# Order of the early gate operands and the first gate sums on VectorE

## The chip, the cores and the metric

The kernel runs on one core of a Trainium2 chip. The metric is the device time of one execution in microseconds, as the median over timed runs; the profile is of one further execution.

## The reference

Two layers of an encoder over 1024 tokens of 1024 features, in float32. Each layer is a token mixer (layer 0: multi-head latent attention, layer 1: differential attention), its output projection, and a SwiGLU part, both with a scaled residual and a layer normalisation:

```python
h = _layernorm(ALPHA * h + mix, ln_mix_g[i], ln_mix_b[i])
h = _layernorm(ALPHA * h + _swiglu(h, ffn_w_gu[i], ffn_w_down[i]), ln_ffn_g[i], ln_ffn_b[i])

def _swiglu(x, w_gu, w_down):
    gate, up = jnp.split(x @ w_gu, 2, axis=-1)
    return (jax.nn.silu(gate) * up) @ w_down
```

The hidden width D_FF is 2816, that is 22 blocks of 128.

## The kernel before

Engines: TensorE (PE in the profile) does the matmuls, VectorE (DVE), ScalarE (ACT) and GpSimd (POOL) the elementwise work, and the sync queue (SP) issues most transfers. Each engine, and the sync queue, takes its instructions in one fixed order. That order is not the order of the text: a planner replays the program against its own model of the durations and puts each instruction at the place where that model has it ready, with priorities (`tc.high_priority`) that lift some. The function `behind(i, j)` adds a constraint for the planner: instruction i comes after j on their engine; it adds no semaphore.

**Operands.** A float32 operand of a matmul is split into a high part (a cast on ScalarE, L503) and a low part (the rest, L504, on VectorE or GpSimd); a product is three matmuls per slice of 128 rows: high by high, high by low, low by high. `op_unit` (L508 on) makes such a pair; pairs turn over six buffers of the pool wp (tags wh and wl, three each), so the cast of a pair waits until TensorE has used up an older one.

**Output projection and normalisation.** The token blocks of 128 are taken in the order 6, 7, 4, 5, 2, 3, 0, 1 (`LAST_ORDER`); in layer 0 by `out_proj`, in layer 1 by the class `OutProj` (`rest`). For each block, `layer_norm` (from L163) makes two means (L166, L167), the squares on ScalarE (L170), the centring on VectorE (L176), the variance (L178), a power on GpSimd (L180), and the scaled and shifted output on VectorE (L183), which the sync queue stores (L184). In layer 1 y and z are one tile, so L176 overwrites what the squares read; in layer 0 they are two.

**Transposed sums.** `raw_x` (L463 on) transposes a finished block on TensorE into two PSUM banks (xTp). For the blocks 0 to 3 it then forms the sums of a Strassen-like scheme: L482 (b12), a copy of the second bank on ScalarE (L483, b22), L484 (b11), L485 and L486 (b21). L482 and L484 read the first bank, L483 and L485 the second. `raw_x` of a block is called after the `layer_norm` of the next; that of the last block, 1, is left over as `pending`, which `ffn` calls.

**Feed-forward part, gate stage.** `ffn` takes the 22 column blocks n of gate and up; with 7 products per block (numbered "1" to "7") in place of 8. Products 1 and 2 use the weights as they are; 3, 5, 6 and 7 use sums of weights. For the first six blocks (npre = 6), products 1 and 2 come early: `load_pre(n)` loads the two weights (tile gp, tag wr, two buffers) and makes the pairs op_gp, the low parts on GpSimd for n = 0 and 1 and on VectorE for n = 2 to 5; `gates(n)` runs the products of n and n+1 (PSUM tile ga, tag s, four banks, which `raw_x` uses too) in the order (n,1), (n+1,1), (n,2), (n+1,2), copies the first out (L608) and applies Silu to the second (L610), which frees the bank. The text goes: load_pre(0) to load_pre(3), gates(0), load(0), load(1) (tile gr, 1 MB each, L558), pending() with high priority, gates(2), the pairs of the transposed sums (t1, b22, t2, t3, t4), load_pre(4), load_pre(5), gates(4). `prepare(n, pr)` (L570 on) makes the operands of the other products from gr: for n = 0 and 1 the first gate sum a21 = a21 + a22 (L580), then a11 (L582), a12 (L584) and s3 (L588), each from the one before, and the pairs op_g. Their products go to the PSUM tiles gc and gb; L628 to L640 add them up.

Buffers that chain transfers to compute: the load of gp for n = 3 waits for the low parts of n = 1 on GpSimd, that for n = 4 for the low parts of n = 2, that for n = 5 for those of n = 3.

## Time and profile before

| | us |
|---|---|
| median of 3 runs | 2288.1 |
| lowest and highest | 2285.23, 2289.94 |
| the profiled execution | 2289.88 |
| its span, first to last instruction | 2288.1 |

Mean granted TensorE clock over the span: 0.997. TensorE is busy for 98% of the span, VectorE 68%, ScalarE 44%, GpSimd 38%.

In a row of a timeline stand the start, the duration, the engine, the line, the operation and its tiles, the number of instructions merged, and in brackets the idle time of the engine ahead of it with what ended that. In a row of the chain of waits stand start, duration, and what ran. In a row of windows stand the stretch, its length, the busy time (and instructions) of PE, PEld, DVE, ACT and POOL, then TensorE's clock, the DMA share and GB/s. Matmuls overlap in their pipeline: one lasts 0.39 us, and at full clock the next starts 0.23 us after it.

### The profile page before, as it was taken

How to read it: one execution, taken by the hardware profiler on the slowest of the kernel's cores; microseconds unless marked ns; L12 is line 12 of the kernel's file. 1: busy time of each engine (PE TensorE's matmuls, PEld its weight loads, DVE VectorE, ACT ScalarE, POOL GpSimd, SP SyncE). 2: the span in 40 equal slices, each digit the busy share in tenths (PEclk: the TensorE clock that was granted, in tenths of full speed). 3: DMA queues.
4: the chain of work that ended last, by engine and by line, in shares of the span. 5: the costliest groups of instructions: out<-in, count | busy, mean ns of one | idle time of the engine just before them, and what ended most of it. 6: DMA issues, size and time to landing. Idle time of an engine off the chain costs nothing.

```text
span 2288.1 us, 31118 instructions
## 1 busy us (share of the span) xinstructions
PE 2245.8 (98%) x11410; PEld 1913.3 (84%) x11410; DVE 1556.8 (68%) x2837; ACT 1015.4 (44%) x2097; POOL 864.0 (38%) x687
## 2 busy tenths in 40 slices
PE   8999999999999999999999999999999999999997
PEld 8999998878888887888889898988778888877886
DVE  5676665686666658677576666676776665668777
ACT  4455564342333324344465655564432333234353
POOL 2232341114444435555432423221024444436563
PEclk9999999999999999999999999999999999999998
DMA  5010125334444428444311212154254131338353
GB/s 201 14 35 31 41 72 198 140 132 151 151 152 179 151 103 331 184 179 149 106 45 31 70 28 66 33 200 155 92 175 143 69 138 69 138 115 317 132 205 119
DMA packets 105544, 288.28 MB, mean 126 GB/s; under 512 B 7968, under 2 KB 30112, under 8 KB 94896
## 3 DMA queue, kind: packets, MB, share of 16 engines
q1 hardware_dynamic: 100976, 275.87, 33.9%
q0 software_dynamic: 4416, 10.42, 1.6%
q8 instruction: 90, 1.47, 0.3%
q14 instruction: 62, 0.51, 0.1%
HBM read 205.00 MB, written 77.07 MB: 123 GB/s over the span
## 4 chain that ended last, share of the span: by engine, by line
PE 90%; DVE 4%; DMA 3%; issue 1%; ACT 1%; POOL 1%; SPq 0%; DVEq 0%; POOLq 0%; ACTq 0%
PE gb L549 14%; PE gc L549 10%; PE ga L549 10%; PE dw L818 7%; PE s_a L219 4%; PE zp_a L417 3%; PE dx L818 3%; PE s_b L219 3%; PE dv L818 3%; PE dy L818 3%; PE bp L145 3%; PE bp L143 3%; PE bp L144 3%; PE o_a L262 2%; PE o_b L262 2%; PE hq L1023 1%
## 5 line engine op out<-in xcount | busy, mean ns | idle before, releaser
L503 ACT CAST op_g<-gr 128x512 fp32r<-128x512 f32 x240 | 146.8, 621 | 370.1 <-PE gb L549 182.3
L504 POOL TENSOR_TENSOR op_g<-gr,op_g 128x512 fp32r<-128x512 f32 x104 | 146.6, 1415 | 247.9 <-ACT op_g L503 139.9
L504 DVE TENSOR_TENSOR op_h<-rh,op_h 128x512 fp32r<-128x512 f32 x154 | 162.5, 1083 | 63.7 <-ACT op_h L503 63.6
L549 PE MATMUL ga<-xh_m,op_g 128*128 128x512 f32 x512 | 168.2, 389 | 0.0
L503 ACT CAST op_h<-rh 128x512 fp32r<-128x512 f32 x154 | 92.9, 620 | 139.7 <-PE dx L818 38.0
L818 PE MATMUL dw<-op_w_t,op_h 128*128 128x512 f32 x660 | 151.3, 390 | 0.0
L818 PEld LDWEIGHTS dw<-op_w_t,op_h 128*128 128x128 f32 x660 | 123.5, 188 | 26.0 <-DVE op_h L504 0.4
L227 ACT ACTIVATE l_b<-l_b,mx_b 128x256 f32<-128x256 f32 (+7 forms) x128 | 99.4, 777 | 76.4 <-DVE mx_b L222 72.4
L818 PE MATMUL dx<-op_w_b,op_h 128*128 128x512 f32 x528 | 122.5, 391 | 7.4 <-ACT op_w_b L503 3.9
L1328 POOL TENSOR_SCALAR l_b<-l_b,rb,cst 128x128 f32<-128x128 f32 (+3 forms) x64 | 52.5, 820 | 204.4 <-DVE rb L1327 193.0
L504 POOL TENSOR_TENSOR op_w_t<-tt,op_w_t 128x512 fp32r<-128x512 f32 x66 | 98.7, 1499 | 80.7 <-ACT op_w_t L503 80.1
L818 PEld LDWEIGHTS dx<-op_w_b,op_h 128*128 128x128 f32 x528 | 98.5, 188 | 31.0 <-ACT op_w_b L503 4.7
L504 DVE TENSOR_TENSOR op_g<-gr,op_g 128x512 fp32r<-128x512 f32 x136 | 110.6, 819 | 14.5 <-ACT op_g L503 14.3
L549 PE MATMUL gb<-t4h_f,op_g 128*128 128x512 f32 x352 | 115.9, 390 | 3.7 <-DVE tmp L632 3.7
L504 POOL TENSOR_TENSOR op_g<-s,op_g 128x512 fp32r<-128x512 f32 x40 | 54.8, 1369 | 170.1 <-ACT op_g L503 161.9
L549 PE MATMUL gb<-t2h_f,op_g 128*128 128x512 f32 x352 | 115.6, 390 | 0.4 <-DVE op_g L504 0.4
L549 PE MATMUL gc<-t1h_f,op_g 128*128 128x512 f32 x352 | 115.6, 389 | 0.1
L549 PE MATMUL gc<-b22h_f,op_g 128*128 128x512 f32 x352 | 115.3, 389 | 0.0
L549 PE MATMUL gb<-t3h_f,op_g 128*128 128x512 f32 x352 | 115.2, 389 | 0.0
L549 PEld LDWEIGHTS ga<-xh_m,op_g 128*128 128x128 f32 x512 | 96.1, 188 | 20.0
L143 PE MATMUL bp<-xT_f,h_wb 128*128 128x512 f32 x256 | 101.7, 397 | 0.0
L144 PE MATMUL bp<-xT_f,h_wb 128*128 128x512 f32 x256 | 101.5, 397 | 0.0
(382 smaller groups left out, 6736.7 us busy)
## 6 DMA issues: line engine op xcount, KB each, us to landing
gr<-in_w_gu SPq DMA_DIRECT2D x44, 1024.0 KB, 6.9
rh<-h_dr SPq DMA_DIRECT2D x28, 1024.0 KB, 5.1
h_dr<-sh SPq DMA_DIRECT2D x22, 1024.0 KB, 5.0
h_dr<-hp SPq DMA_DIRECT2D x22, 768.0 KB, 4.1
tt<-in_w_dn SPq DMA_DIRECT2D x22, 512.0 KB, 8.0
rh<-h_dr SPq DMA_DIRECT2D x14, 768.0 KB, 4.4
wo_dr<-op_pwo SPq DMA_DIRECT2D x16, 512.0 KB, 3.5
z<-xs_dr SPq DMA_DIRECT2D x16, 512.0 KB, 10.2
```

The source lines that it names most:

```text
L143: T.matmul(ps_out, lh, rh, start=(i == 0), stop=False)
L144: T.matmul(ps_out, lh, rl, start=False, stop=False)
L145: T.matmul(ps_out, ll, rh, start=False, stop=(i == n - 1))
L219: T.matmul(s[:, :w], lh, rh[:, ks], start=(j == 0), stop=(j == len(q_pass) - 1))
L227: ends["exp"] = A.activation(l[:, :n], l[:, :n], AF.Exp, bias=mx, scale=-1.0, accum_out=sm).ins
L262: T.matmul(po[:, c], a, b[:, j % 2, c], start=st, stop=sp_, skip_group_check=True)
L417: T.matmul(m, a[:, h, :], self.wo[h][w][:, c], start=(start and h == heads[0] and a is oh and w == 0), stop=(stop and h == heads[-1] and a ...
L503: A.copy(hi, src)
L504: return eng.tensor_tensor(lo, src, f32(hi), ALU.subtract).ins
L549: T.matmul(o, w[:, a, kc], x[b][:, k, :], start=(first and k == 0 and (a, b) == (0, 0)), stop=(k == 3 and a == 1), skip_group_check=True,)
L818: T.matmul(o, h[:, a, c], w[:, b_], start=(first and (a, b_) == (0, 0)), stop=(last and a == 1), skip_group_check=True,)
L1328: G.tensor_scalar(l1[:, :n], l1[:, :n], r[:, 1:2], nlam, ALU.mult, ALU.mult)
```

## The change

Three constraints are added, all on VectorE; no instruction is added or removed. The low parts of op_gp for n = 2 come after the centring (L176) of the last output block; those for n = 3, 4 and 5 after that block's final normalised output (L183); the first gate sums (L580) of n = 0 and 1 after that block's last transposed sum (L486). Both layers run this code.

```diff
@@ layer_norm
         centred = V.scalar_tensor_tensor(y, z, nmu[:, 1:2], g, ALU.add, ALU.mult)
+        ends["centred"] = centred.ins
...
-            V.scalar_tensor_tensor(y[:, c], y[:, c], rs, b[:, c], ALU.mult, ALU.add)
+            ends["ln"] = V.scalar_tensor_tensor(y[:, c], y[:, c], rs, b[:, c], ALU.mult, ALU.add).ins
@@ raw_x
-            V.tensor_tensor(b21, b21, b12, ALU.add)
+            ends["x"] = V.tensor_tensor(b21, b21, b12, ALU.add).ins
@@ load_pre
             for i, pr in enumerate("12"):
                 ops[n, pr] = op_unit(t[:, i], eng, f"gp{layer}_{n}_{pr}")
+                if eng is V:
+                    behind(turns["last"], ends["centred" if n == 2 else "ln"])
@@ prepare
             if pr == ("5" if n < 2 else "6"):
-                V.tensor_tensor(a21, a21, a22, ALU.add)
+                i = V.tensor_tensor(a21, a21, a22, ALU.add).ins
+                if n < 2:
+                    behind(i, ends["x"])
```

## Prediction

> **What bounds the kernel now.** I read the page first, then the chain of work that ended last, then the timelines of TensorE, VectorE, ScalarE, GpSimd and the sync queue at the two places that the diff touches: the start of the feed-forward part in layer 0 (about 440 us) and in layer 1 (about 1627 us).

> ```profile
> span 2288.1 us, 31118 instructions
> PE 2245.8 (98%) x11410; PEld 1913.3 (84%) x11410; DVE 1556.8 (68%) x2837; ACT 1015.4 (44%) x2097; POOL 864.0 (38%) x687
> ```

> TensorE is the bound. An edit that adds and removes no instruction can only change its idle time and the speed at which it runs. The profiled execution took 2289.88 us; the median of the three timed runs is 2288.1, 1.78 below, and what I work out is carried over as a difference. TensorE's timeline at the two places and, last, a row of the chain for its normal pace:

> ```profile
> 442.39 0.48 PE L549 MATMUL ga<-xh_m,op_gp 128*128 128x512 f32 x1
> 454.16 0.48 PE L549 MATMUL ga<-xh_m,op_gp 128*128 128x512 f32 x1
> 499.58 0.50 PE L549 MATMUL gb<-t4h_f,op_g 128*128 128x512 f32 x1 [1.41 <-DVE tmp L632]
> ...
> 1627.78 0.48 PE L549 MATMUL ga<-xh_m,op_gp 128*128 128x512 f32 x1
> 1635.67 1.06 PE L148 MATMUL xTp_a<-ident,z_a 128*128 128x128 f32 x8 [2.19 <-DVE z_a L183]
> 1641.82 0.39 PE L549 MATMUL ga<-xh_m,op_gp 128*128 128x512 f32 x1
> 1644.73 0.70 PE L549 MATMUL ga<-xh_m,op_gp 128*128 128x512 f32 x1 [2.52 <-DVE xr_m L484]
> 1691.81 0.50 PE L549 MATMUL gb<-t4h_f,op_g 128*128 128x512 f32 x1 [1.66 <-DVE tmp L632]
> ```
> ```profile
> 510.80 5.44 PE gb L549 x24
> ```

> The same work, first gate product to first gb<-t4h, takes 499.58 - 442.39 = 57.2 us in layer 0 and 1691.81 - 1627.78 = 64.0 us in layer 1. In layer 0 TensorE waits once (1.41 us, at its end); in layer 1 three times, and the first two are not in layer 0. So layer 1 has some 6.8 us to give, layer 0 at most 1.4. The chain names what the second wait hangs on:

> ```profile
> 1635.92 6.75 DMA gr<-in_w_gu
> 1642.69 0.03 DVE gr L580
> ...
> 1643.30 0.68 DVE op_gp L504
> 1643.98 0.61 DVE xr_m L484
> ...
> 1644.73 18.66 PE ga L549 x74
> ```

> VectorE runs its instructions in order. The first gate sum (L580) stands ahead of L484, and its operand is a 1 MB load that lands 6.75 us after its issue. L484 is the last block's transposed sum; it reads the PSUM bank that the next gate product (n=2) takes. So a sum that nobody needs yet holds back the bank that TensorE needs now. After the gap TensorE is slow as well: at the pace of 5.44 / 24 = 0.227 us the 74 matmuls would take 16.8 us, and they took 18.66, of which 0.16 is the last one's own end; 1.7 us is lost speed. The windows show it as granted clock:

> ```profile
> 445.00:455.00 10.00, 10.00 (x50) 8.38 (x49) 8.49 (x14) 7.29 (x14) 0.55 (x1) 1.00 0.95 367
> 500.00:510.00 10.00, 10.00 (x46) 8.23 (x45) 9.11 (x12) 1.35 (x3) 4.60 (x4) 1.00 0.31 105
> 1646.00:1650.00 4.00, 4.00 (x14) 3.13 (x13) 4.00 (x8) 3.97 (x7) 0.00 (x0) 0.72 0.00 0
> ```

> (The last three columns are clock, DMA share, GB/s.) The clock is 0.72 after the 2.52 us gap and 1.00 after layer 0's 1.41 us gap.

> **The change part by part.** It adds order on VectorE alone. I write (n,p) for operand p of gate block n.

> *Low parts of n=2 behind the centring (L176).* The rows of layer 1, VectorE, then ScalarE, GpSimd (one of layer 0 last):

> ```profile
> 1628.65 2.03 DVE L504 TENSOR_TENSOR op_gp<-gp,op_gp 128x512 fp32r<-128x512 f32 x2
> 1630.60 0.68 DVE L484 TENSOR_TENSOR xr_m<-xr_m,xTp_a 128x512 f32<-128x512 f32 x1
> ...
> 1631.80 1.27 DVE L176 SCALAR_TENSOR_TENSOR z_a<-z_a,nmu_a,gb 128x1024 f32<-128x1024 f32 x1
> ...
> 1633.12 0.68 DVE L486 TENSOR_TENSOR xr_m<-xr_m,xr_m 128x512 f32<-128x512 f32 x1
> 1634.24 1.28 DVE L183 SCALAR_TENSOR_TENSOR z_a<-z_a,rs_a,gb 128x1024 f32<-128x1024 f32 x1 [0.44 <-POOL rs_a L180]
> ```
> ```profile
> 1629.57 0.68 ACT L170 ACTIVATE zp_a<-z_a,nmu_a 128x512 f32<-128x512 f32 x1
> ...
> 1635.97 0.63 ACT L503 CAST op_gp<-gp 128x512 fp32r<-128x512 f32 x1 [1.08 <-DMA gp<-in_w_gu]
> 1636.77 0.58 ACT L483 COPY xr_m<-xTp_a 128x512 f32<-128x512 f32 x1 [0.17 <-PE xTp_a L148]
> ```
> ```profile
> 1626.98 2.55 POOL L504 TENSOR_TENSOR op_gp<-gp,op_gp 128x512 fp32r<-128x512 f32 x2 [6.28 <-ACT op_gp L503]
> 1633.27 0.93 POOL L180 TENSOR_TENSOR rs_a<-ve_a,cst 128x1 f32<-128x1 f32 x1 [3.74 <-DVE ve_a L178]
> ```
> ```profile
> 447.81 0.55 POOL L180 TENSOR_TENSOR rs_a<-ve_a,cst 128x1 f32<-128x1 f32 x1 [4.59 <-DVE ve_a L178]
> ```

> The two low parts take 2.03 us in front of L484, L485 and L176. Without them L176, which overwrites z, may start when the second square (1629.57 + 0.68 = 1630.25) is done: 1630.3, not 1631.80, 1.5 us earlier. From there the row distances stay (L183 2.44 after L176, transposes 1.43 after L183): L183 at 1632.8, transposes at 1634.2. The first 24 gate products end at 1627.78 + 5.44 = 1633.2, so the first wait shrinks from 2.19 to about 0.8. Bounds: 0 if the low parts fill VectorE ahead of L183 again, 2.2 if the wait goes entirely. I take 1.5.

> GpSimd's power (L180), which L183 waits for, took 0.93 us where L486 had started beside it and 0.55 in layer 0. The moved low parts now stand near it. [...]

> *n=3, 4 and 5 behind the output of the normalisation (L183).* In layer 1 no VectorE low part of these stands ahead of L183; in layer 0 one does. Cost nothing: TensorE takes n=2 and 3 only after 48 products of n=0 and 1.

> *The first gate sums behind the last transposed sum (L486).* The last product before the second wait starts at 1641.82; one pace later, at 1642.05, TensorE is free, 6.4 us after the transposes began. With the transposes at 1634.2 it is free at 1640.6. L483 starts 1.1 us after the transposes, as now, and L484 behind it is done by 1636.8, far ahead of 1640.6. So the second wait goes: 1642.05 to 1644.73 is 2.7 us. The lost speed, 1.7 us, goes with it. L580 then stands on VectorE behind L486, near 1638, and its load, issued on the sync queue right behind L183's store, lands at 1635.92 - 1.5 + 6.75 = 1641.2: VectorE may still stand 3.2 us there. Behind it stand the low parts of (3,2) and n=4; TensorE takes (3,2) three products of 12 matmuls (half of 5.44 us each) after 1640.6, at 1648.8. That slack covers the stall.

> *Sum for layer 1:* 1.5 + 2.7 + 1.7 = 5.9 us of the 6.8 that separate the layers.

> *The loads behind the moved low parts.* The tile of n=2 is freed by its low parts; the load of n=4 waits for it on the sync queue, so it moves too. In layer 0:

> ```profile
> 443.24 0.89 SPq L564 DMA_DIRECT2D gp<-in_w_gu  x2
> ```
> ```profile
> DMA to landing us min/median/max: 3.4/4.6/8.0
> ```
> ```profile
> 448.67 0.62 ACT L503 CAST op_gp<-gp 128x512 fp32r<-128x512 f32 x1
> ...
> 450.84 0.62 ACT L503 CAST op_gp<-gp 128x512 fp32r<-128x512 f32 x1 [1.55 <-PE ga L549]
> ...
> 452.78 0.60 ACT L610 ACTIVATE pg<-ga 128x512 f32<-128x512 f32 x1
> ```
> ```profile
> 442.60 1.17 DVE L504 TENSOR_TENSOR op_gp<-gp,op_gp 128x512 fp32r<-128x512 f32 x1
> ...
> 445.73 1.27 DVE L176 SCALAR_TENSOR_TENSOR y_a<-zy_a,nmu_a,mg 128x1024 f32<-128x1024 f32 x1
> ...
> 451.17 0.69 DVE L580 TENSOR_TENSOR gr<-gr 128x512 f32<-128x512 f32 x1 [0.69 <-DMA gr<-in_w_gu]
> ...
> 460.93 0.69 DVE L486 TENSOR_TENSOR xr_m<-xr_m,xr_m 128x512 f32<-128x512 f32 x1
> ...
> 469.36 0.69 DVE L504 TENSOR_TENSOR op_g<-gr,op_g 128x512 fp32r<-128x512 f32 x1
> ```

> The n=4 load goes from about 443.8 (the end of the instruction at 442.60) to about 447.2 at the earliest (L176's end at 447.0, less the 1.17 us that leave its front, and two low parts of 0.69), behind the two 1 MB gate loads; the DMA engines are 0.95 busy at 367 GB/s from 445 to 455, and the 2.5 MB ahead of it then take 6.8 us, its own 0.5 MB 1.4: landing near 453.2. If its cast (448.67 now) waits on ScalarE behind nothing that matters, this costs nothing, and I take that; TensorE wants n=4 only 48 products (10.9 us) after 454.16. If the cast keeps its place, see the first rival. In layer 1 L176 ends at 1631.6, the load is issued near 1633 and lands by the median at 1637.6; even a cast ahead of L483 then leaves L484 done by 1640.1, in time.

> In layer 0 the first sums move from 451.17 behind L486. Seven instructions that now run before L486 has ended (two each of L580, L582 and L584, one L588), by 0.69 us 4.8 us, change places with the last block's sums, which come earlier; the total stays. Bounds: a gain of 1.4 (the wait at 499.58 goes) and a loss of 4.8 (all of it on the path). I take 0, since TensorE has no wait there before 499.58.

> Forecast: 2288.1 - 5.9 = 2282.2 us, its own range 2280 to 2284 (the profiled execution: 2284.0).

> **The rivals.**

> *ScalarE stands on the n=4 load in layer 0.* If its cast stays ahead of the next cast and of the first Silu (452.78), ScalarE resumes at 453.2 and owes the distance of the rows, 452.78 - 448.67 less the 1.55 us for which it then waited for TensorE, 2.6 us, and 0.6 for the Silu: 456.4. The product at 454.16 needs the bank that this Silu frees: 2.3 us of wait, and by the row of the 2.52 us gap 1.7 us of slow clock as well. Result 2284.5 to 2286.2. For it: the cast now stands there. Against it: the planner sees the load move too. [...]

> *The waits before gb<-t4h go too.* They end on VectorE's L632, held up by the same kind of sums; if the new order has VectorE ahead there, 1.4 + 1.7 us more: 2279.1. Against it: both layers show that wait although they came to it differently.

> *No change.* The planner puts other instructions that wait, n=4's low part for one, where L580 stood, and L484 is as late as now: 2288, within 2 us.

> *Slower: VectorE becomes the bound of the first sums' products.* The seven sums (4.8 us) come after L486, and in layer 1 VectorE stands on the load there, in order, with every operand of the gate stage behind it. The first low part of a gate sum's operand is written at 469.36 in layer 0, and no row shows slack between it and its product. Were it 4.8 us late, TensorE would wait 4.8 and lose 1.7 of speed in layer 0, and in layer 1 the wait would only move, its 5.9 given back: 2288.1 + 6.5 = 2294.6. It decides where TensorE has no other product to take. The gate products of n=0 to 5, 144 matmuls at 0.227 us, and a block's transposes (about 1 us) would last to about 476 in layer 0, over 6 us beyond 469.36; so it needs an order that puts the sums' products ahead of those of n=5.

> **How the numbers follow.** Forecast 0.44, the ScalarE rival 0.24, both late waits gone 0.10, no change 0.11, slower 0.11. About 0.2% (4.6 us) is what a measurement of this kernel can tell from no change, so faster begins at 2283.5: most of the forecast, the 2279.1 case and a sliver of the first rival, 0.52. Same: the rest of these and the no-change case, 0.36. Slower: 0.12. The range 2278.5 to 2288.0 leaves out the slower case and the upper half of no change.

> **What would show it.** Right: in layer 1 L580 behind L486; L484 about 2.5 us after the transposes start; no wait of TensorE for L484; clock 1.00 throughout; a first wait under 1 us; first gate product to first gb<-t4h near 58 us. Wrong: a cast of op_gp on ScalarE ahead of L610 or L483 waiting for its load; TensorE waiting for op_g low parts; layer 0's stretch over 58 us; or the stretches as they are, in which case the sums were not what held the bank.

## The result, and the profile after

The changed kernel takes 2283.73 us (median of 21 runs, 2282.23 to 2286.71), the kernel before, timed beside it, 2286.5 us (21 runs, 2285.05 to 2289.94). The ratio is 0.9987, 95% interval 0.9981 to 0.9993: 2.8 us faster, about half of the 5.9 us of the forecast, and within 0.2%. The profiled execution after took 2282.89 us; that of before, 2289.88, lay 3.4 us above its kernel's median, so the two spans are not subtracted. The page after, its first lines (span, then busy time by engine):

```profile
span 2281.0 us, 31129 instructions
...
PE 2244.4 (98%) x11410; PEld 1914.0 (84%) x11410; DVE 1556.9 (68%) x2837; ACT 1015.6 (45%) x2097; POOL 864.3 (38%) x687
```

The diff shifts the lines behind L176 by 1 to 5: L183 is L184, L484 to L486 are L485 to L487, L503 and L504 are L504 and L505, L580 is L583, L588 is L593, L608 and L610 are L613 and L615, L630 and L632 are L635 and L637.

The same places on TensorE's timeline after: layer 0 (the first row and the second), then layer 1.

```profile
442.57 0.48 PE L550 MATMUL ga<-xh_m,op_gp 128*128 128x512 f32 x1
...
498.19 0.50 PE L550 MATMUL gb<-t4h_f,op_g 128*128 128x512 f32 x1
...
1626.59 0.48 PE L550 MATMUL ga<-xh_m,op_gp 128*128 128x512 f32 x1
...
1633.96 0.50 PE L550 MATMUL ga<-xh_m,op_gp 128*128 128x512 f32 x1 [1.68 <-ACT pg L613]
...
1636.87 1.03 PE L148 MATMUL xTp_a<-ident,z_a 128*128 128x128 f32 x8
...
1646.88 0.50 PE L550 MATMUL ga<-xh_m,op_gp 128*128 128x512 f32 x1 [0.80 <-ACT op_gp L504]
...
1648.36 0.50 PE L550 MATMUL ga<-xh_m,op_gp 128*128 128x512 f32 x1 [0.75 <-ACT pg L613]
...
1687.64 0.50 PE L550 MATMUL gb<-t4h_f,op_g 128*128 128x512 f32 x1 [1.35 <-DVE tmp L637]
```

Both waits that the prediction named in layer 1 are gone: the transposes (1636.87) and the product for which the bank was held no longer wait for VectorE. The windows after show the clock at the place where it was 0.72 (the third number from the end):

```profile
1646.00:1650.00 4.00, 2.45 (x10) 1.68 (x10) 4.00 (x8) 3.84 (x8) 0.00 (x0) 1.00 0.00 0
```

But TensorE is busy for only 2.45 of these 4 us, at full clock. There are three new waits, and all of them name ScalarE. They stand near the places of the old ones: 1.68 us after the same 24 products, where 2.19 stood, and 0.80 and 0.75 us behind the transposes, where 2.52 stood. The stretch from the first gate product to the first gb<-t4h went from 64.03 to 1687.64 - 1626.59 = 61.05 us, where the forecast had 58. The chain of waits after shows what holds it (start, duration, what ran):

```profile
1625.79 2.55 POOL op_gp L505 x2
1628.35 4.38 DMA gp<-in_w_gu
1632.85 0.48 issue
1633.33 0.59 ACT pg L613
1633.92 0.04 issue
1633.96 3.08 PE ga L550 x12
1637.06 0.62 ACT op_gp L504
...
1638.99 0.60 ACT pg L615
1639.59 0.48 ACT xr_m L484
...
1642.04 2.19 ACT b22h_f L504 x4
1644.22 1.91 ACT t3h_f L504 x4
...
1646.82 0.50 ACT pg L615
...
1647.83 0.49 ACT pg L613
1648.32 0.04 issue
1648.36 6.19 PE ga L550 x26
```

A load of gp leads to ScalarE's copy of a gate product, though the copy has nothing to do with that load. ScalarE's timeline tells why: the cast of the pair (3,1) stands ahead of the two copies.

```profile
1632.81 0.62 ACT L504 CAST op_gp<-gp 128x512 fp32r<-128x512 f32 x1 [3.64 <-DMA gp<-in_w_gu]
1633.33 1.07 ACT L613 COPY pg<-ga 128x512 f32<-128x512 f32 x2
```

The kernel before has the same order:

```profile
1633.30 0.62 ACT L503 CAST op_gp<-gp 128x512 fp32r<-128x512 f32 x1 [2.94 <-DMA gp<-in_w_gu]
1633.83 1.06 ACT L608 COPY pg<-ga 128x512 f32<-128x512 f32 x2
```

There it cost nothing: TensorE stood for the transposes until 1635.67, and the copies were done by 1634.9. With the first wait gone, this cover is gone, and the copies, which free the banks for the next products, are what is late next. From 1637.06 on ScalarE has some 11 us of work with hardly a pause (the Silu's table, the casts of t1, b22 and t3), so its lateness comes back at 1646.88 and 1648.36.

Executions differ in parts far from the edit: the first gate product of layer 0 came between 440.4 and 442.6 us over the profiled executions of all kernels here, and at 440.44 and 441.90 in two executions of one kernel, so a difference of one span by under 2 us is no evidence. The stretches below leave that part out. They are worked out as above, for layer 0 from its own two rows.

| | layer 0 stretch | layer 1 stretch | time, ratio to before |
|---|---|---|---|
| before, two executions | 57.19, 56.95 | 64.03, 63.79 | 0.9998 (0.9989 to 1.0007) |
| after, two executions | 55.62, 56.84 | 61.05, 61.36 | 0.9987 (0.9978 to 0.9995) |
| only the sums' order | 55.39 | 62.81 | 0.9978 (0.9968 to 0.9987) |
| only the low parts' order, two | 55.39, 55.39 | 61.40, 60.70 | 0.9976 (0.9966 to 0.9986), 0.9979 (0.9970 to 0.9987) |
| order in layer 1 alone | 56.98 | 60.85 | 0.9988 (0.9979 to 0.9996) |
| after, and the cast (3,1) moved, two | 56.83, 55.64 | 57.64, 57.67 | 0.9965 (0.9952 to 0.9979), 0.9971 (0.9959 to 0.9982) |
| only the cast moved | 57.46 | 65.63 | 1.0001 (0.9992 to 1.0009) |

### The profile page after: what moved, and what is told of

Read it like the earlier page. It is cut to its first block, busy times and chain, and to the rows that moved or that the text cites. A ratio compares the mean times of both kernels' runs of the same rounds, so it can differ in the third digit from the quotient of the medians.

```text
span 2281.0 us, 31129 instructions
## 1 busy us (share of the span) xinstructions
PE 2244.4 (98%) x11410; PEld 1914.0 (84%) x11410; DVE 1556.9 (68%) x2837; ACT 1015.6 (45%) x2097; POOL 864.3 (38%) x687
## 3 DMA queue, kind: packets, MB, share of 16 engines
q8 instruction: 90, 1.47, 0.3%
## 4 chain that ended last, share of the span: by engine, by line
PE 92%; DVE 3%; ACT 1%; DMA 1%; issue 1%; POOL 1%; SPq 0%; DVEq 0%; POOLq 0%; ACTq 0%
PE gb L550 15%; PE gc L550 10%; PE ga L550 10%; PE dw L823 7%; PE dx L823 5%; PE s_a L220 4%; PE zp_a L418 3%; PE s_b L220 3%; PE dv L823 3%; PE dy L823 3%; PE bp L145 3%; PE bp L143 3%; PE bp L144 3%; PE o_a L263 2%; PE o_b L263 2%; PE hq L1028 1%
## 5 line engine op out<-in xcount | busy, mean ns | idle before, releaser
L504 ACT CAST op_g<-gr 128x512 fp32r<-128x512 f32 x240 | 147.1, 621 | 373.8 <-PE gb L550 184.4
L505 POOL TENSOR_TENSOR op_g<-gr,op_g 128x512 fp32r<-128x512 f32 x104 | 145.2, 1401 | 248.4 <-ACT op_g L504 139.6
L505 DVE TENSOR_TENSOR op_h<-rh,op_h 128x512 fp32r<-128x512 f32 x154 | 166.4, 1110 | 61.3 <-ACT op_h L504 61.3
L504 ACT CAST op_h<-rh 128x512 fp32r<-128x512 f32 x154 | 92.7, 619 | 136.2 <-PE dx L823 38.9
L505 POOL TENSOR_TENSOR op_w_t<-tt,op_w_t 128x512 fp32r<-128x512 f32 x66 | 100.4, 1525 | 75.0 <-ACT op_w_t L504 69.9
L505 DVE TENSOR_TENSOR op_g<-gr,op_g 128x512 fp32r<-128x512 f32 x136 | 110.6, 818 | 15.3 <-ACT op_g L504 15.1
L505 POOL TENSOR_TENSOR op_g<-s,op_g 128x512 fp32r<-128x512 f32 x40 | 54.8, 1369 | 168.8 <-ACT op_g L504 160.7
```

Of the source, the lines that this page charges most:

```text
L504: A.copy(hi, src)
L505: return eng.tensor_tensor(lo, src, f32(hi), ALU.subtract).ins
```

## The experiments

**The kernels before and after, once more,** for the spread of the stretches and of the times.

> The kernel before once more, for a second profile and for what the comparison gives when nothing differs. If the prediction's ledger rests on something that every execution has, layer 1 takes 64.0 us again from its first gate product to the first gb<-t4h (layer 0: 57.2), with TensorE waits of 2.2 and 2.5 us and a lower clock behind them. If the slow clock depends on when the gap falls, layer 1 takes about 62.3 us this time, and the forecast counted 1.7 us that most executions don't have. Ratio 1.000 either way.

> The changed kernel once more. Theory A (a wait that the change uncovers): on ScalarE the cast of n=3 waits for its load ahead of the copies of the first gate products, and TensorE waits 1.7 us for a copy in layer 1 in this profile as well; layer 1 takes 61.1 us over the stretch, layer 0 55.6, ratio about 0.9985. Theory B (noise of single profiles): the waits behind the copies differ from profile to profile by as much as they are long.

Measured: 2286.45 and 2283.5 us, beside 2286.87 for the kernel before on that chip. The slow clock of layer 1 was there again in the second execution before (0.71 to 0.72 from 1643 to 1649) and not in either execution after. Layer 0's late wait was 1.4 us in both executions before, and none and 1.1 us in those after.

**One half of the change at a time.** The other constraint is left out:

```diff
 # sums: without the low parts' order
-                    behind(turns["last"], ends["centred" if n == 2 else "ln"])
+                    pass
...
 # low: without the sums' order
-                    behind(i, ends["x"])
+                    pass
```

> Only the first gate sums are ordered behind the last transposed sum; the low parts are free as before. Theory A: the sums alone remove the second wait and the slow clock of layer 1 (2.7 + 1.7 us), the first wait (2.2) stays, and the cast of n=3 stays hidden under that first wait, so layer 1 takes about 59.6 us over the stretch, less than the 61.1 of the whole change; ratio 0.9975 to 0.9985. Rival (the low parts are needed too, since n=4's low part now stands ahead of L484 in place of L580): layer 1 stays above 62 us, ratio 0.999 to 1.000.

> Only the low parts are ordered behind the normalisation; the sums are free as before. Theory A: L580 still stands ahead of L484 and waits for its load, so the second wait stays, the first shrinks by up to 1.5 us: layer 1 takes 62.5 to 64 us over the stretch, ratio 0.9993 to 1.000. Rival (the low parts carry the gain): layer 1 at or below 61.5 us, ratio 0.9985 or less.

Measured: 2281.82 and 2282.11 us; neither is slower than both together. With the sums' order alone the first wait stays and the second is gone. TensorE's first wait, and VectorE around the last transposed sum, in that kernel:

```profile
1631.69 1.06 PE L148 MATMUL xTp_a<-ident,z_a 128*128 128x128 f32 x8 [2.18 <-DVE z_a L184]
```
```profile
1635.96 0.69 DVE L487 TENSOR_TENSOR xr_m<-xr_m,xr_m 128x512 f32<-128x512 f32 x1
1638.54 0.69 DVE L583 TENSOR_TENSOR gr<-gr 128x512 f32<-128x512 f32 x1 [1.89 <-DMA gr<-in_w_gu]
```

The clock was 1.00 from 1636 to 1655. Later in the stretch TensorE waits three times for operands and sums of the gate stage (1.6, 1.3 and 1.0 us), so part of the gain is given back there: theory A had the wait that goes and the time, but its 59.6 us of the stretch became 62.81. With the low parts' order alone, the planner put the first sum behind the last transposed sum by itself, so the rival was right there and theory A wrong. TensorE and VectorE in that kernel:

```profile
1630.26 1.06 PE L148 MATMUL xTp_a<-ident,z_a 128*128 128x128 f32 x8 [1.47 <-ACT pg L613]
...
1643.15 0.50 PE L550 MATMUL ga<-xh_m,op_gp 128*128 128x512 f32 x1 [0.92 <-ACT pg L615]
```
```profile
1636.97 0.68 DVE L487 TENSOR_TENSOR xr_m<-xr_m,xr_m 128x512 f32<-128x512 f32 x1
1639.06 0.69 DVE L583 TENSOR_TENSOR gr<-gr 128x512 f32<-128x512 f32 x1 [1.40 <-DMA gr<-in_w_gu]
```

So the halves do not add: either removes the second wait and the slow clock, because moving one thing made the planner order the rest anew.

**The low half again,** since its first gate product had come 1.8 us early.

> The kernel with only the low parts ordered, once more, unchanged. Theory A (the first 440 us, which are 1.8 us shorter there than in the kernels before and after, belong to that program): first gate product at 440.4 us again, 4 to 5 us faster than before. Rival B (they belong to how one load or run of it started): first gate product at 442.1-442.6 us as in the others, 2.5 to 3.5 us faster than before.

Measured: 2282.21 us; the first gate product at 441.90 us. The early start was that execution's, as rival B had it; the ratio stayed, as theory A had it. What makes this kernel 4.6 us faster than before is then mostly in the two stretches: 1.6 to 1.8 us in layer 0, where it has no late wait, and 2.4 to 3.3 in layer 1.

**The order in layer 1 alone.** `and layer == 1` is added to both conditions of the diff.

> The order is added in layer 1 alone; layer 0 has the order of the kernel before. Theory A (layer 1 gives the whole gain): stretch of layer 0 57.0 us as before, of layer 1 61.1-61.4 us, time within 0.5 us of the changed kernel. Rival B (the late wait for a sum in layer 0, 1.4 us before, is part of the gain): layer 0 stretch 57.0-57.2 where the changed kernel has 55.6-56.8, time 0.5 to 1.4 us above the changed kernel's.

Measured: 2283.39 us, the same as the changed kernel's. Layer 0 has its late wait of 1.4 us and a stretch of 56.98; what layer 0 gives in the changed kernel is too little or too changeable for the time to show. The run does not hold layer 1 fixed, though: TensorE's order there is not the changed kernel's but that of the kernel with the low parts alone, with waits of 1.47 us at the transposes and 0.94 behind them.

**The uncovered cast.** The changed kernel, with the cast of (3,1) ordered behind the copies in layer 1 (for that, its `load_pre` is called after `gates(0)`); TensorE's order stays.

```diff
+                if n == 3 and layer:
+                    behind(turns["cast"], ends["p1"])     # p1: the copy of (1,1) out of ga
...
-        for n in range(4):
+        for n in range(4 - layer):
             load_pre(n, G if n < 2 else V)
         gates(0)
+        if layer:
+            load_pre(3, V)
```

> The changed kernel with one cast moved: in layer 1 ScalarE's cast of the operand (3,1) stands behind the two copies of the first gate products instead of ahead of them; TensorE's order is the changed kernel's. Theory A (the copies came late only because that cast waited 3.64 us for its load): TensorE's wait of 1.7 us for the copies goes, the first gate stretch of layer 1 falls from 61.1-61.4 to 59.4-59.7 us, the kernel is 1.7 us faster than the changed one (about 2281.8 us by the median of the changed kernel). Rival B (VectorE's queue behind the last transposed sum is the limit, and TensorE only meets it earlier or later): the 1.7 us come back as longer waits for the sums of the first products (now 1.4 us in all), the stretch stays at 60.8-61.4 us, no change. Between the two: VectorE stands 1.15 us for TensorE ahead of those sums, so a part of up to 1.2 us would be kept.

Measured: 2279.13 us, and layer 1 took 57.64 us: 3.4 to 3.7 less than in the changed kernel, twice what theory A gave for the one wait. TensorE's waits there, and ScalarE's two copies, which now follow the products:

```profile
1625.55 0.48 PE L550 MATMUL ga<-xh_m,op_gp 128*128 128x512 f32 x1
...
1633.82 1.03 PE L148 MATMUL xTp_a<-ident,z_a 128*128 128x128 f32 x8
...
1643.91 0.50 PE L550 MATMUL ga<-xh_m,op_gp 128*128 128x512 f32 x1 [0.43 <-ACT pg L615]
...
1683.19 0.50 PE L550 MATMUL gb<-t4h_f,op_g 128*128 128x512 f32 x1 [1.35 <-DVE tmp L641]
```
```profile
1628.57 0.59 ACT L615 COPY pg<-ga 128x512 f32<-128x512 f32 x1 [0.43 <-PE ga L550]
1631.29 0.59 ACT L615 COPY pg<-ga 128x512 f32<-128x512 f32 x1 [2.13 <-PE ga L550]
1631.77 0.63 ACT L504 CAST op_gp<-gp 128x512 fp32r<-128x512 f32 x1
```

(Here L615 is the copy and L641 the sum that was L637.) The wait of 1.68 is gone, and of the two behind it, 1.55 together, 0.43 is left: they were the same lateness, passed on by ScalarE's queue. VectorE's rival is out for this part: the wait for its sum at the end of the stretch stayed at 1.35 and did not grow.

**The same again, and the cast alone** (without the change's constraints).

> The changed kernel with the cast moved, once more, unchanged, beside the others on one chip. Theory A (the 3.7 us that its layer 1 stretch is shorter belong to the program): stretch 57.6 us again, 6 to 8 us faster than before, ratio 0.9965 to 0.9975. Rival B (a part of it was that run): stretch 59.4 us or more, ratio 0.998 or more.

> The kernel before (no order on VectorE's low parts and first sums) with the one cast of layer 1 moved behind the two copies of the first gate products. Theory A (in the kernel before the cast was covered: it and the copies ended at 1633.3-1634.9 us while TensorE waited for the last output block's normalisation until 1635.7 us anyway): layer 1 stretch 63.8-64.2 us as before, no change of the time. Rival B (the cast's place alone is what costs, the order on VectorE is not needed): the stretch falls to near the 57.6 us of the kernel with both, the time by 4 to 6 us.

Measured: 2279.99 us with a stretch of 57.67, so the gain belongs to the program; and 2287.47 us, no gain, for the cast alone, whose stretch is even 1.6 us longer, which neither theory had. TensorE there:

```profile
1635.64 1.06 PE L148 MATMUL xTp_a<-ident,z_a 128*128 128x128 f32 x8 [2.17 <-DVE z_a L184]
...
1645.84 0.76 PE L550 MATMUL ga<-xh_m,op_gp 128*128 128x512 f32 x1 [3.67 <-DVE xr_m L485]
```
```profile
1646.00:1650.00 4.00, 4.00 (x10) 3.13 (x11) 4.00 (x8) 2.91 (x6) 0.00 (x0) 0.50 0.00 0
```

The first wait is as before; a second sum (L589) now stood on VectorE ahead of L485 as well, the second wait grew from 2.52 to 3.67 us, and the clock fell to 0.50. Only change and cast together bring the 6.1 to 6.4 us of the stretch.

**Two attempts at more.** *low3*: only the low parts ordered, and the cast of (3,1) behind ScalarE's copy L484 (`load_pre(3)` called after `pending()`). *best*: as the kernel with the cast moved, but the sums' order in layer 1 alone (`if n < 2 and layer:`).

> Only the low parts ordered, and in layer 1 the cast of the operand (3,1) behind ScalarE's copy of the last transposes; in that kernel the cast waits 3.12 us for its load and holds the copy, and with it the last transposed sum and VectorE's low parts. Theory A (that cast holds the stretch here too): the sum comes about 1.0 us earlier, TensorE's late waits (0.9, 0.8 and 0.8 us) shrink by about 1.0 in all, layer 1 stretch from 61.4 to 60.4 us. Rival B (the load for the first gate sum, 8.5 us long, is what VectorE waits for next, 1.4 us): the sum is earlier but the wait for the load grows by as much, stretch 61.2-61.6 us, no change.

> As the kernel with the cast moved, but the first gate sums ordered behind the transposed sums in layer 1 alone, so that layer 0 has only the order of its low parts (its stretch was 55.4 us in each run that had this, against 56.8 with both). Theory A (the stretches add): layer 0 55.4, layer 1 57.6 us, 1.4 us faster than the kernel with the cast moved, 8 to 9 us faster than before. Rival B (the planner, whose order of layer 1 also hangs on layer 0, loads gp(4) ahead of the first two 1 MB loads there again, as it did without the order on the sums in layer 0): layer 0 55.4, layer 1 60.7-61.4 us, 2 us slower than the kernel with the cast moved.

Measured for low3: 2283.57 us (0.9987, 0.9978 to 0.9996), layer 1 62.72 us, over what either theory gave. The expectation took the wrong cast: the one that waits 3.12 us in the kernel with the low parts alone (at 1633.31) belongs to n=4, whose load was issued at 1628.99; that of (3,1) is the one at 1628.60. The move still let the copy run ahead of both, and the last transposed sum came 11.5 us after the first gate product in place of 13.9. But the first gate sum came 16.0 us after it in both, since VectorE now waited 3.17 us for its load in place of 1.40: rival B's mechanism. The stretch grew as well, as VectorE's later work came late: TensorE waited 0.5 us for a low part of op_gp that VectorE wrote at 1650.95, and the late waits grew to 1.4 and 1.1. For best: 2281.3 us (0.9974, 0.9963 to 0.9986), layer 0 55.39, layer 1 60.03. Rival B, nearly to its size. The sync queue of best has both gp loads (L565) ahead of the 1 MB ones (L559), and TensorE waits for the transposes again:

```profile
1626.19 4.48 SPq L565 DMA_DIRECT2D gp<-in_w_gu  x2
1631.49 0.33 SPq L185 DMA_DIRECT2D xs_dr<-z_a  x1
1631.86 1.49 SPq L559 DMA_DIRECT2D gr<-in_w_gu  x2
```
```profile
1631.60 1.06 PE L148 MATMUL xTp_a<-ident,z_a 128*128 128x128 f32 x8 [1.48 <-DVE z_a L184]
```

A constraint that is missing in layer 0 changed the order in layer 1. The lowest medians of the study are those of the changed kernel with the cast moved, 2279.1 and 2280.0 us; by time alone the intervals do not part it from best or from the kernels with one half of the change, by the stretch of layer 1 it stands apart, with 57.6 us against 60.0 and more.

## Why the prediction was right or wrong

- *The number.* In part luck. The 2283.73 lies inside the forecast's own 2280 to 2284 because the forecast starts from the median of three runs, 2288.1; from that of 21, 2286.5, the same 5.9 us would have given 2280.6. As a difference, 2.8 of 5.9 us came, and the time falls just short of the 2283.5 from which the prediction called it faster.
- *The bound and the place.* Right. TensorE sets the time, and the largest gain in either stretch came in layer 1.
- *The second wait and the lost speed (2.7 and 1.7 us).* Right in the mechanism: no wait for L485, and clock 1.00 at that place, in every kernel with either half of the change. Not in the size: 1.55 us of other waits stand behind the transposes after. The 1.7 us were there in both profiled executions before, but a wait does not bring them in every run (last section). That it took only the sums' order was wrong: the low parts' order alone did it too.
- *The first wait (1.5 of 2.19 us).* (2.19 - 1.5 leaves 0.7; the prediction wrote about 0.8.) The centring came earlier as worked out (2.61 us after the first gate product, 4.02 before). The normalised output did not follow at the old distance: the two low parts of n=2 slipped in between (L184 3.13 us after L176, not 2.44). The transposes did not wait for it, because the planner also moved them behind 36 gate products in place of 24, and their wait went altogether; but the product that now stands in their place waited 1.68 us. GpSimd's power took 0.93 us again and ended at 1631.62, ahead of L184 at 1632.33, so its length cost nothing here.
- *The step that failed* is the one that let the first wait shrink with nothing late next to it, together with "Cost nothing" for n=3. It looked at VectorE's low parts of n=3 and not at ScalarE's cast of the same pair, which stood for its load ahead of the copies of the first products, covered by the wait that was to go. A cast of op_gp that waits for its load ahead of L610 was among the prediction's own signs of being wrong. Uncovered, it cost the stretch 3.4 to 3.7 us, as moving it showed with TensorE's order unchanged. With the cast out of the way layer 1 went from 64.03 to 57.64, 6.4 us, against the 5.9 of the sum.
- *The first sums' load.* The prediction had VectorE stand up to 3.2 us there. In the kernel after there is no stand: the planner issued the 1 MB loads at 1628.73, ahead of the normalised output's store and not behind it, and the sum ran at 1643.11 right behind L487. In the kernel with the sums' order alone, where the loads stayed behind, it stood 1.89.
- *Layer 0 at nothing.* Roughly right for the time. The late wait was none to 1.1 us in four executions with the whole change (with and without the cast moved), so the rival in which these waits go came true in part there, and hardly in layer 1 (1.66 to 1.35 us).
- *ScalarE on the n=4 load in layer 0.* The load was issued at 447.24, as worked out (447.2). The stand did not happen: the cast moved behind the Silu, as the text against it said. The same mechanism happened with another cast in the other layer. ScalarE in layer 0 after, where the cast at 451.08 waits for TensorE alone and the two at 454.25 stand behind the Silu:

```profile
451.08 0.62 ACT L504 CAST op_gp<-gp 128x512 fp32r<-128x512 f32 x1 [2.19 <-PE ga L550]
451.72 1.28 ACT L615 ACT_TABLE_LOAD   x1
453.01 1.33 ACT L615 ACTIVATE pg<-ga 128x512 f32<-128x512 f32 x2
454.25 1.13 ACT L504 CAST op_gp<-gp 128x512 fp32r<-128x512 f32 x2
```

- *Slower.* VectorE did become what sets the last step of the stretch (it is in the chain from 1678.16 to 1687.60 after), at 1.35 us of TensorE's time, no more than before.
- *Left open:* why the kernels with one half of the change are as fast as or faster than with both is explained by the stretch of layer 0 only in part. The down projection of layer 1 was also 1.2 to 1.5 us shorter in the executions after (with the cast alone too, and less in one with the cast moved). Most of that is a wait of TensorE for VectorE's low parts of op_h, 1.57 and 1.55 us in the executions before (at 2084), 0.67 and none in those after, 0.45 with the cast alone, 1.75 in that one with the cast moved; why it differs is not known.

## What to carry to other kernels

When a wait goes, list every instruction that was late beneath it on all engines, with its own queue: what an in-order engine holds ahead of the next thing that the bound engine needs becomes the new wait (here 1.68 us), and its lateness is paid again wherever that queue has no slack (here 1.55 us). A constraint for a planner is not a local edit: read the whole new order, of both layers, before adding up gains, and test a combination rather than adding its halves. One added constraint on the uncovered instruction shortened the stretch here by 3.4 to 3.7 us, the change itself by 2.4 to 3.0.

## What the runs showed of the hardware that was not expected

One short wait can bring the slow clock, and the same wait can leave it alone. Ahead of the down projection of layer 0 TensorE waits once for 1.95 us, in every execution here. In the execution after, the clock behind it was 0.50; in the second execution of the same kernel it stayed at 1.00 (a row of TensorE and one of the windows for each):

```profile
866.12 9.20 PE L823 MATMUL dx<-op_w_b,op_h 128*128 128x512 f32 x32 [1.95 <-ACT op_w_b L504]
866.70:870.00 3.30, 3.30 (x9) 2.63 (x8) 3.27 (x3) 1.19 (x3) 3.14 (x3) 0.50 0.93 286
```
```profile
867.06 3.92 PE L823 MATMUL dx<-op_w_b,op_h 128*128 128x512 f32 x16 [1.95 <-ACT op_w_b L504]
867.10:871.00 3.90, 3.88 (x16) 2.88 (x16) 3.87 (x4) 2.38 (x4) 3.53 (x3) 1.00 0.95 307
```

One step of 3.41 us at 0.50 costs 1.7 us, the lost speed of the prediction. By the 1.85 us above, a wait of 2.52 us would bring it in some two runs of three (an estimate: it escapes when a boundary falls more than 0.67 us from both of its ends, 1.18 of 3.41 us), so a run of the kernel before would lose some 1.1 us by it on average.
